# Expert weights of a mixture-of-experts block fetched by row pairs and row halves, with transposes that read every second column

## The chip, the cores and the metric

The kernel runs on one core of a Trainium2 chip. The metric is the device time of one execution in microseconds (us), taken as the median of three runs. One of the executions was also recorded by the hardware profiler; that profile and its trace are what is read here.

## What is computed

One decoder block over 512 tokens of 1024 features in float32: a norm, a pooling mixer and a gated linear recurrence side by side, an output projection, and then a mixture of experts. Each token goes to 2 of 16 experts. The last part of the reference, cut to what matters here:

```
for e in range(N_EXP):                                    # 16 experts
    he = silu(xt @ e_gate[e]) * (xt @ e_up[e])            # (512 x 1024) @ (1024 x 512), twice
    y = y + comb[:, e:e + 1] * (he @ e_down[e])           # (512 x 512) @ (512 x 1024)
x = x + y;  return rms_norm(x, norm_f_g)
```

`comb` is zero for the tokens that an expert does not get. The three matrices of an expert are 2 MB each, 96 MB for all of them.

## The kernel before

The work is done in three stages: the mixers (to about 280 us of the span), the output projection with the router (to about 370 us), and the experts (from there to the end). The change is in the experts.

**Weights.** All weights come as chunks of 1 MB, in one fixed order: gate of expert e, down of expert e-1, up of expert e. `add` (L98) describes a chunk, `load_raw` (L138) issues its load on SyncE's queue, at most 14 chunks ahead and with at most three in flight (a load waits for the landing of the third one before it). A chunk of gate or up is 512 rows of 512 columns, a chunk of down is all 512 rows of 512 of the 1024 columns; in both each partition gets four rows of 512 numbers, and each row is a run of 2 KB in memory.

**Splits.** TensorE works on float32r parts, so each half of a chunk (128 x 1024) is split in two: ScalarE casts it to the high part (`split`, L151) and VectorE subtracts that from the original, for the low part (L152). `weights` (L159) decides where in program order a split stands: three halves ahead of its use (`SPLIT_AHEAD`), and one ahead from expert 12 on (`LATE_AHEAD`).

**One expert.** The tokens of an expert sit on the 128 partitions. The loop at L791 runs, for expert e: the first half of gate e; four transposes of the hidden rows of expert e-1 (`h_parts`); the second half of gate e; `down(e - 1)`; `next_x(e + 1)`, eight transposes of the gathered rows of the next expert (`x_parts`, L713, into the tile xt); `up(e)`. Each product is three matmuls per 128 rows of weights: high by high, high by low, low by high (L726 to L728). In a matmul the tokens' tile is the stationary operand and the weights are the moving one; in a transpose the rows xg are the stationary operand and the identity is the moving one.

**Down.** `down` (L769) makes the two column halves of the result one after the other: twelve matmuls into bank py0, then ScalarE's scaled copy of py0 into y (L774), then twelve into py1 and its copy, then a scatter by GpSimd that adds y to the tokens' rows in memory. For the last expert `down` is replaced by code of its own, with the same order of halves (L890). The very last steps read the rows back, add the last expert's part, norm and store.

Each engine runs its instructions in the order in which the builder put them. Names below carry the expert (y4, py4_0) or the chunk (w60_1 is the second half of chunk 60).

Of the kernel before, what the change touches and what calls it, by code (L numbers as in the profile page):

```python
# [17 lines left out]
P = 128  # L18
S = 512
D = 1024  # L20
KD = D // P
# [8 lines left out]
DE = 512  # L30
# [6 lines left out]
def tile_hybrid_block(  # L37
# [28 lines left out]
    def bank(name):  # L66
        return psum.tile([P, 512], F32, tag="ps", name=name)
# [2 lines left out]
        return sb.tile(shape, dtype, tag=name.split("_")[0] + "_t", name=name, bufs=bufs)  # L70

    class Feat:
        """[P, KD, S] in two tiles."""

        def __init__(self, dtype, name):
            self.t = [b8([P, KD // 2, S], dtype, f"{name}{i}") for i in range(2)]
# [15 lines left out]
    tbl = tc.dram_tile([S * NE, 1], I32, name="slot_ids")  # L92
    tblw = tc.dram_tile([S * NE, 1], F32, name="slot_w")

# [1 line left out]
    chunks = []  # L96

    def add(w, r0, rows, c0, n):  # L98
        chunks.append((w[r0:r0 + rows, c0:c0 + n].rearrange("(k p) n -> p k n", p=P), rows // P, n))
        return len(chunks) - 1  # L100

    def z_chunks(base, cols):
        return [add(w_in, 0, D, base + 256 * i, 256) for i in range(cols // 256)]
# [12 lines left out]
    c_g, c_u, c_d = {}, {}, {}  # L116

    def add_exp(dst, w, e, down):
        dst[e] = [add(w[e], 0, 512, 512 * i, 512) if down else add(w[e], 512 * i, 512, 0, DE)
                  for i in range(2)]  # L120

    for e in range(NE):
        add_exp(c_g, e_gate, e, False)
# [14 lines left out]
    def load_raw(upto, after=None):  # L138
        while nxt["raw"] <= min(upto, len(chunks) - 1):
            j = nxt["raw"]  # L140
            ap, kk, n = chunks[j]
            raws[j] = b8([P, kk, n], F32, f"raw{j}")
            loads[j] = SP.dma_start(raws[j], ap).ins
            if j - IN_FLIGHT in loads:
                tc.add_manual_dep(loads[j], loads[j - IN_FLIGHT].name, SYNC, reason="loads in flight")
            if after is not None:
                tc.add_manual_dep(loads[j], after.name, SYNC, reason="loads yield to it")
            nxt["raw"] += 1
# [19 lines left out]
        load_raw((nxt["split"] - 1) // 2 + raw_ahead)  # L168
        return pairs[c]

# [1 line left out]
    x_rows = [s4([P, D], F32, f"x_rows{t}") for t in range(NT)]  # L172
    for t in range(NT):
        SP.dma_start(x_rows[t], xr[t * P:(t + 1) * P, :])
# [3 lines left out]
        SP.dma_start(raws[0][:, 4 * h:4 * h + 4], ap0[:, 4 * h:4 * h + 4])  # L178
    nxt["raw"] = 1

# [1 line left out]
    ident = const.tile([P, P], F32, name="ident")  # L182
    make_identity(nc, ident)
    mhalf = const.tile([P, 1], F32, name="mhalf")
# [21 lines left out]
    g1, lam, cb, br, bi, psc, g2f = (par[n] for n in ("g1", "lam", "cb", "br", "bi", "psc", "g2f"))  # L206
    cw = par["cw"].rearrange("p (j c) -> p j c", j=4)

# [1 line left out]
    def rstd_of(src, name):  # L210
        sq = s2([P, D], BF16, f"sq_{name}")
        ssum = tiny([P, 1], F32, f"ssum_{name}", 4)
# [37 lines left out]
            mm3(ps, w[:, 0], w[:, 1], hi[k], lo[k], k == 0, k == kk - 1)  # L250
        return ps

# [1 line left out]
    sp8 = const.tile([P, KD], F32, name="sp8")  # L254
    nsp8 = const.tile([P, KD], F32, name="nsp8")

    def softplus():
        def small(name):
            return tiny([P, KD], F32, name, 1)

        nlam, mab, ee, den, ss, s2_, acc = (small(n) for n in
                                            ("nlam", "mab", "ee", "den", "ssr", "ssq", "sacc"))
        DVE.tensor_scalar(nlam, lam, -1.0, None, op0=ALU.mult)
        DVE.tensor_tensor(mab, lam, nlam, op=ALU.min)
        ACT.activation(ee, mab, AF.Exp)
        DVE.tensor_scalar(den, ee, 2.0, None, op0=ALU.add)
        DVE.reciprocal(den, den)
        DVE.tensor_tensor(ss, ee, den, op=ALU.mult)
        DVE.tensor_tensor(s2_, ss, ss, op=ALU.mult)
        DVE.tensor_scalar(acc, s2_, 1.0 / 19.0, 1.0 / 17.0, op0=ALU.mult, op1=ALU.add)  # L270
        for k in (15, 13, 11, 9, 7, 5, 3, 1):
            DVE.tensor_tensor(acc, acc, s2_, op=ALU.mult)
            DVE.tensor_scalar(acc, acc, 1.0 / k, None, op0=ALU.add)
        DVE.tensor_tensor(acc, acc, ss, op=ALU.mult)
        DVE.tensor_scalar(nlam, nlam, 0.0, None, op0=ALU.max)
        DVE.scalar_tensor_tensor(acc, acc, 2.0, nlam, op0=ALU.mult, op1=ALU.add)
        DVE.tensor_scalar(sp8, acc, 8.0, None, op0=ALU.mult)
        DVE.tensor_scalar(nsp8, acc, -8.0, None, op0=ALU.mult)

# [1 line left out]
    ra, ix, uu = Lazy(F32, "ra"), Lazy(F32, "ix"), Lazy(F32, "uu")  # L281
    bd = []

# [45 lines left out]
            lru_gates(*pend.pop(0))  # L329
        pend.append(lru_conv(c, ps))  # L330

# [1 line left out]
    icnt = const.tile([P, PAD], F32, name="icnt")  # L333
    for j in range(PAD):
        POOL.memset(icnt[:, j:j + 1], 1.0 / (j + 1))
# [70 lines left out]
                ACT.copy(yh[cc], uu[cc])  # L406
                DVE.tensor_tensor(yl[cc], uu[cc], yh[cc].bitcast(F32), op=ALU.subtract)

# [1 line left out]
    m = Lazy(F32, "m")  # L410
    for j in range(KD):
        wp = weights(c_ga[j // 2], 4, 2)
# [13 lines left out]
        ps = feat_block(wp, (j % 2) * P, KD, xh, xl, f"zgb{j}")  # L426
        ACT.activation(sgb[j], ps, AF.Sigmoid)

# [1 line left out]
    NR = 2 * NG + NE  # L430
    rw = s2([P, KD, NG + NE], F32, "rw")
    POOL.dma_start(rw[:, :, :NG], router_group_w[0].rearrange("(k p) n -> p k n", p=P))
# [63 lines left out]
            ACT.copy(mt[i][:, 0, j, :], mj)  # L496
            DVE.tensor_tensor(mt[i][:, 1, j, :], mj, mt[i][:, 0, j, :].bitcast(F32), op=ALU.subtract)

# [1 line left out]
    x2s, h2s, xts, xpart, xg = {}, {}, {}, [], []  # L500

    def evac4(tp, hi, lo):
# [16 lines left out]
    def route(t):  # L519
# [75 lines left out]
        for e0, e1 in ((0, 2), (2, NE)) if last else ((0, 1), (1, NE)) if t == NT - 2 else ((0, NE),):  # L595
            for e in range(e0, e1):
                DVE.tensor_scalar(ohs[:, e, :], slot1, pm[:, e:e + 1], None, op0=ALU.is_equal)
                PE.matmul(spv[:, e, :3], ohs[:, e, :], idp[:, t, e, :3], start=True, stop=True)
            if last and e0 == 0:
                oh0 = s2([P, P], F32, "oh0")  # L600
                DVE.tensor_scalar(oh0, slot1, pm[:, 0:1], None, op0=ALU.is_equal)
                tps = [bank(f"xtp0_{hf}") for hf in range(2)]
                for d in range(KD):
                    PE.matmul(tps[d // 4][:, d % 4 * P:(d % 4 + 1) * P], h2s[t][:, d * P:(d + 1) * P], oh0,
                              start=True, stop=True)
            ac = slacc[:, e0:e1, :3]
            DVE.tensor_tensor(ac, ac, spv[:, e0:e1, :3], op=ALU.add)
            if t == NT - 2 and e0 == 0:
                slot_rows(rows0, e0, e1)
            if last:  # L610
                done = slot_rows(rows[:, e0:e1], e0, e1)
                if e0 == 0:
                    gather(rows[:, 1:2], xg[1])
                    with tc.issue_after(done):
                        for hf, tp in enumerate(tps):
                            hs = slice(hf * 4, hf * 4 + 4)
                            DVE.tensor_tensor(xpart[hf], tp, xpart[hf], op=ALU.add)
                            evac4(xpart[hf], xts[0][:, 0, hs, :], xts[0][:, 1, hs, :])
                    yield
# [76 lines left out]
    for hf in range(2):  # L696
        tp = bank(f"xg0t{hf}")
        for q in range(4):
            d = hf * 4 + q
            PE.transpose(tp[:, q * P:(q + 1) * P], xg[0][:, d * P:(d + 1) * P], ident)  # L700
        xpart.append(s2([P, 512], F32, f"xpart{hf}"))
        ACT.copy(xpart[hf], tp)
    xg.append(s4([P, D], F32, "xg1"))
# [9 lines left out]
    def x_parts(src, xt, nm, tp2=None):  # L713
        for hf in range(2):
            tp = bank(f"xtp{nm}_{hf}") if tp2 is None else tp2
            for q in range(4):
                d = hf * 4 + q
                PE.transpose(tp[:, q * P:(q + 1) * P], src[:, d * P:(d + 1) * P], ident)  # L718
            evac4(tp, xt[:, 0, hf * 4:hf * 4 + 4, :], xt[:, 1, hf * 4:hf * 4 + 4, :])

    def tok_mm(ps, xt, j0, wp, first, last):
        for k in range(4):
            if k % 2 == 0:
                w = wp(k // 2)
            hi, lo = xt[:, 0, j0 + k, :], xt[:, 1, j0 + k, :]
            PE.matmul(ps, hi, w[:, 0, k % 2, :], start=first and k == 0, stop=False)  # L726
            PE.matmul(ps, hi, w[:, 1, k % 2, :], start=False, stop=False)  # L727
            PE.matmul(ps, lo, w[:, 0, k % 2, :], start=False, stop=last and k == 3)  # L728

    def hidden(pg, pu, nm):  # L730
        sg = s2([P, DE], F32, f"silu{nm}")
# [36 lines left out]

    def down(e, ht):  # L769
        yt = s4([P, D], F32, f"y{e}")  # L770
        for n in range(2):
            py = bank(f"py{e}_{n}")
            tok_mm(py, ht, 0, exp_w(c_d[e], n), True, True)
            ACT.activation(yt[:, n * 512:(n + 1) * 512], py, AF.Copy, scale=wslot[:, e:e + 1])  # L774
            yield
        scatter_add(rows[:, e:e + 1], yt)

    def gate_half(e, pg, i):
        tok_mm(pg, xts[e], 4 * i, exp_w(c_g[e], i), i == 0, i == 1)

# [1 line left out]
    cn = bank("cn")  # L782
    PE.matmul(cn[:, :NE], ones, acum, start=True, stop=True)
    nmf = const.tile([P, 1], F32, name="nmf")
# [4 lines left out]
    L = NE - 1  # L789
# [26 lines left out]
    for i in range(2):  # L816
        weights(c_d[L][i], 0, 0)

# [1 line left out]
    n_max = nc.values_load(nmi[0:1, 0:1], min_val=0, max_val=S)  # L820
    with tc.If(n_max > P):
        emp = s2([P, S * NE // P], I32, "emp")
# [16 lines left out]
        with tc.For_i(0, NE, 1) as ie:  # L839
            with tc.For_i(P, S, P) as iq:  # L840
# [14 lines left out]

                def part(w, r0, c0):
                    src = w[bass.ds(ie, 1), r0:r0 + 512, c0:c0 + 512]
                    SP.dma_start(r, src.rearrange("o (k p) n -> p (o k) n", p=P))
                    for h in range(2):
                        split(r[:, 2 * h:2 * h + 2], ow[h][:, 0], ow[h][:, 1])  # L860
                    return lambda h: ow[h]
# [11 lines left out]
                    ACT.activation(og[:, n * 512:(n + 1) * 512], ps, AF.Copy, scale=wsl)  # L873
                scatter_add(sl, og)

# [1 line left out]
    xb = [b8([P, 2, D], F32, f"xb{i}") for i in range(2)]  # L877
    for t in range(NT):
        SP.dma_start(xb[t // 2][:, t % 2, :], xd[t * P:(t + 1) * P, :])  # L879
# [7 lines left out]
    xv = [[xb[t // 2][:, t % 2, n * 512:(n + 1) * 512] for n in range(2)] for t in range(NT)]  # L887
    frs = []
    py = [bank(f"py{L}_{n}") for n in range(2)]
    for n in range(2):  # L890
        tok_mm(py[n], ht, 0, exp_w(c_d[L], n), True, True)
    yp = [s4([P, 2, 512], F32R, f"yp{n}") for n in range(2)]
    for n in range(2):
        ACT.activation(yp[n][:, 0], py[n], AF.Copy, scale=wslot[:, L:L + 1])
# [56 lines left out]
```

## Time and profile before

| | |
|---|---|
| median of three runs | 697.42 us (696.87 to 699.47) |
| span of the profiled execution | 695.7 us |
| granted TensorE clock, mean | 0.977 |
| TensorE busy, share of the span | 94% |
| VectorE, ScalarE busy | 72%, 62% |
| moved by DMA | 153.23 MB |

The span goes from the first instruction to the last; the profiled execution has no other time of its own, and the span is 1.7 us under the median. Busy shares of TensorE are of limited use, because matmuls overlap each other in the record: a matmul of 512 columns is shown for 0.39 us and the next one begins 0.23 us after it. Whether it runs densely is read from the distance of the starts.

### The profile page before, as it was taken

The numbers are of one execution on the slowest core, as the hardware profiler recorded it, in microseconds if no ns is written. First come the engines' busy times: TensorE is split into PE (matmuls) and PEld (weight loads), VectorE is DVE, ScalarE is ACT, GpSimd is POOL, SyncE is SP. The second block draws the span as 40 slices with busy tenths as digits, with TensorE's granted clock in tenths as the row PEclk, the third lists the DMA queues.
The fourth block names the chain that finished last, engine by engine and source line by source line (L and its number), as shares of the span: only waits on it lengthen the run. The fifth ranks groups of instructions, "written<-read, shape, count | busy, mean of one in ns | idle before, by whom it ended". The sixth has DMA issues, their size and how long they took to land. (4 is left out here: it accounts for less than half of the span.)

```text
span 695.7 us, 8405 instructions
## 1 busy us (share of the span) xinstructions
PE 650.9 (94%) x3044; PEld 526.8 (76%) x3044; DVE 502.5 (72%) x792; ACT 431.4 (62%) x579; POOL 79.6 (11%) x101
## 2 busy tenths in 40 slices
PE   5999999999999999999959999999999999999970
PEld 4888888788888888887747787777777777777850
DVE  6886699952322227556687898898899888887946
ACT  6599957752213225141244888888888888777913
POOL 3000000000100000000131111111111111101013
PEclk9999999999999999999988999999999999999996
DMA  7920323213217113696584999999999999999134
GB/s 215 345 79 20 127 81 118 95 62 122 65 62 241 53 69 121 235 389 236 198 310 134 334 333 342 341 351 338 331 337 336 361 336 342 335 339 365 53 98 161
DMA packets 88053, 153.23 MB, mean 220 GB/s; under 512 B 7250, under 2 KB 29894, under 8 KB 88009
## 3 DMA queue, kind: packets, MB, share of 16 engines
q1 hardware_dynamic: 81736, 138.98, 57.5%
q0 software_dynamic: 5824, 12.64, 6.8%
q10 hardware_dynamic: 448, 1.05, 0.4%
q8 instruction: 24, 0.39, 0.2%
q14 instruction: 21, 0.16, 0.1%
HBM read 146.67 MB, written 14.16 MB: 231 GB/s over the span
## 5 line engine op out<-in xcount | busy, mean ns | idle before, releaser
L152 DVE TENSOR_TENSOR w<-raw,w 128x1024 fp32r<-128x1024 f32 x248 | 293.6, 1220 | 69.7 <-ACT w L151 67.6
L151 ACT CAST w<-raw 128x1024 fp32r<-128x1024 f32 x248 | 249.7, 1051 | 59.4 <-DVE w L152 14.1
L727 PE MATMUL pu<-w,xt 128*128 128x512 f32 x128 | 51.9, 406 | 2.3 <-DVE w L152 2.3
L726 PE MATMUL pu<-w,xt 128*128 128x512 f32 x128 | 52.2, 408 | 1.8 <-ACT w L151 1.8
L726 PE MATMUL pg<-w,xt 128*128 128x512 f32 x128 | 52.8, 412 | 1.1
L727 PE MATMUL py<-w,ht 128*128 128x512 f32 x128 | 51.6, 403 | 0.0
L728 PE MATMUL py<-w,ht 128*128 128x512 f32 x128 | 50.7, 396 | 0.6 <-DVE ht L505 0.6
L728 PE MATMUL pg<-w,xt 128*128 128x512 f32 x128 | 50.4, 394 | 0.5 <-DVE xt L505 0.5
L728 PE MATMUL pu<-w,xt 128*128 128x512 f32 x128 | 50.7, 396 | 0.0
L727 PE MATMUL pg<-w,xt 128*128 128x512 f32 x128 | 50.3, 393 | 0.3 <-DVE w L152 0.3
L508 POOL DMA_INDIRECT xg<-h_rows,rows x16 | 26.9, 1679 | 197.6 <-PE xtp L718 177.8
L726 PE MATMUL py<-w,ht 128*128 128x512 f32 x128 | 48.8, 395 | 0.8 <-ACT ht L504 0.8
L743 POOL DMA_INDIRECT x_acc<-y,rows x15 | 24.6, 1639 | 62.9 <-ACT y L774 36.4
L727 PEld LDWEIGHTS pu<-w,xt 128*128 128x128 f32 x128 | 24.5, 191 | 8.8 <-DVE w L152 3.2
L726 PEld LDWEIGHTS pg<-w,xt 128*128 128x128 f32 x128 | 24.1, 188 | 9.4 <-ACT w L151 5.3
L726 PEld LDWEIGHTS pu<-w,xt 128*128 128x128 f32 x128 | 24.3, 190 | 7.7 <-ACT w L151 3.1
L726 PEld LDWEIGHTS py<-w,ht 128*128 128x128 f32 x128 | 24.5, 191 | 6.1 <-ACT ht L504 1.0
L505 DVE TENSOR_TENSOR xt<-xtp,xt 128x512 fp32r<-128x512 f32 x30 | 19.4, 686 | 13.4 <-ACT xt L504 13.4
L727 PEld LDWEIGHTS pg<-w,xt 128*128 128x128 f32 x128 | 24.1, 188 | 6.2 <-DVE w L152 0.7
L728 PEld LDWEIGHTS py<-w,ht 128*128 128x128 f32 x128 | 24.4, 191 | 5.7 <-DVE ht L505 1.0
L728 PEld LDWEIGHTS pg<-w,xt 128*128 128x128 f32 x128 | 24.0, 188 | 5.8 <-DVE xt L505 1.1
L728 PEld LDWEIGHTS pu<-w,xt 128*128 128x128 f32 x128 | 24.5, 191 | 4.8
(292 smaller groups left out, 1414.6 us busy)
## 6 DMA issues: line engine op xcount, KB each, us to landing
raw<-in_exp_w_gate_dram SPq DMA_DIRECT2D x32, 1024.0 KB, 8.0
raw<-in_exp_w_up_dram SPq DMA_DIRECT2D x32, 1024.0 KB, 7.9
raw<-in_exp_w_down_dram SPq DMA_DIRECT2D x32, 1024.0 KB, 10.7
raw<-in_w_in_dram SPq DMA_DIRECT2D x17, 1024.0 KB, 7.7
raw<-in_proj_b_dram SPq DMA_DIRECT2D x4, 1024.0 KB, 9.3
raw<-in_w_out_dram SPq DMA_DIRECT2D x4, 1024.0 KB
x_rows<-in_x_dram SPq DMA_DIRECT2D x4, 512.0 KB
xrow<-in_x_dram SPq DMA_DIRECT2D x4, 512.0 KB
```

What stands on the lines that cost most here:

```text
L151: ACT.copy(hi, r)
L152: DVE.tensor_tensor(lo, r, hi.bitcast(F32), op=ALU.subtract)
L505: DVE.tensor_tensor(lo, tv, hi.bitcast(F32), op=ALU.subtract)
L508: return POOL.indirect_dma_start(out=dst, out_offset=None, in_=h2d[:n, :], in_offset=bass.IndirectOffsetOnAxis(ap=idx, axis=0), bounds_che ...
L726: PE.matmul(ps, hi, w[:, 0, k % 2, :], start=first and k == 0, stop=False)
L727: PE.matmul(ps, hi, w[:, 1, k % 2, :], start=False, stop=False)
L728: PE.matmul(ps, lo, w[:, 0, k % 2, :], start=False, stop=last and k == 3)
L743: POOL.indirect_dma_start(out=xd, out_offset=bass.IndirectOffsetOnAxis(ap=idx, axis=0), in_=src, in_offset=None, bounds_check=S - 1, oob_i ...
```

## The change

Four things change, in the experts alone. A chunk of gate or up is read so that a partition takes two neighbouring rows at a time, 4 KB in one run (`pairs_of`), twice per chunk. So the rows of weights that meet in one matmul are now every second one of a block of 256, and the tokens' features have to be in the same order: `x_cols` reads every second column of xg in each transpose, and of the router's h2 in one matmul per block. A chunk of down is now 256 rows of all 1024 columns, again 4 KB runs. And since a chunk of down then holds half of the rows for both halves of the result, `down` fills py0 and py1 together, chunk by chunk (`down_mm`), and ScalarE's two copies come after all of it.

```
+    def pairs_of(w):
+        return w.rearrange("(j p t) n -> p j (t n)", p=P, t=2)
+    def x_cols(src, d):
+        return src[:, d // 2 * 2 * P + d % 2:d // 2 * 2 * P + 2 * P:2]
...
-        dst[e] = [add(w[e], 0, 512, 512 * i, 512) if down else add(w[e], 512 * i, 512, 0, DE)
-                  for i in range(2)]
+        dst[e] = []
+        for i in range(2):
+            if down:
+                dst[e].append(add(w[e], 256 * i, 256, 0, D))
+            else:
+                chunks.append((pairs_of(w[e][512 * i:512 * i + 512]), 4, DE))
+                dst[e].append(len(chunks) - 1)
...
-                PE.transpose(tp[:, q * P:(q + 1) * P], src[:, d * P:(d + 1) * P], ident)
+                PE.transpose(tp[:, q * P:(q + 1) * P], x_cols(src, d), ident)
...
+    def down_mm(pys, ht, i, wp):
+        for q in range(2):
+            w = wp(q)
+            k = 2 * i + q
+            for n, ps in enumerate(pys):
+                hi, lo = ht[:, 0, k, :], ht[:, 1, k, :]
+                w_h, w_l = (w[:, j, 0, n * 512:(n + 1) * 512] for j in range(2))
+                PE.matmul(ps, hi, w_h, start=k == 0, stop=False)
+                PE.matmul(ps, hi, w_l, start=False, stop=False)
+                PE.matmul(ps, lo, w_h, start=False, stop=k == 3)
...
     def down(e, ht):
         yt = s4([P, D], F32, f"y{e}")
-        for n in range(2):
-            py = bank(f"py{e}_{n}")
-            tok_mm(py, ht, 0, exp_w(c_d[e], n), True, True)
+        pys = [bank(f"py{e}_{n}") for n in range(2)]
+        for i in range(2):
+            down_mm(pys, ht, i, exp_w(c_d[e], i))
+            if i == 0:
+                yield
+        for n, py in enumerate(pys):
             ACT.activation(yt[:, n * 512:(n + 1) * 512], py, AF.Copy, scale=wslot[:, e:e + 1])
-            yield
         scatter_add(rows[:, e:e + 1], yt)
...
-    for n in range(2):
-        tok_mm(py[n], ht, 0, exp_w(c_d[L], n), True, True)
+    for i in range(2):
+        down_mm(py, ht, i, exp_w(c_d[L], i))
```

On TensorE, in loop 5 of the experts, these rows of the kernel before are the middle of `down(4)` (w58 and w59 are the two chunks of its weights):

```order
L726 MATMUL py4_0_3932<-w58_1_3911,ht4_3903 128x512
L726 MATMUL py4_1_3954<-w59_0_3920,ht4_3903 128x512
L727 MATMUL py4_0_3932<-w58_1_3911,ht4_3903 128x512
L728 MATMUL py4_0_3932<-w58_1_3911,ht4_3903 128x512
L726 MATMUL py4_0_3932<-w58_1_3911,ht4_3903 128x512
L727 MATMUL py4_0_3932<-w58_1_3911,ht4_3903 128x512
L728 MATMUL py4_0_3932<-w58_1_3911,ht4_3903 128x512
L727 MATMUL py4_1_3954<-w59_0_3920,ht4_3903 128x512
L728 MATMUL py4_1_3954<-w59_0_3920,ht4_3903 128x512
L726 MATMUL py4_1_3954<-w59_0_3920,ht4_3903 128x512
```

py4_0 is complete after 13 of the 24 matmuls of down. In the changed kernel the end of `down(4)` on TensorE reads like this, up to the first matmul of up (pu5):

```order
L753 MATMUL py4_0_3932<-w59_1_3934,ht4_3903 128x512
L753 MATMUL py4_1_3933<-w59_1_3934,ht4_3903 128x512
L734 MATMUL xtp6_0_3980<-ident_81,xg0_2905 128x128 x4
L754 MATMUL py4_0_3932<-w59_1_3934,ht4_3903 128x512
L755 MATMUL py4_0_3932<-w59_1_3934,ht4_3903 128x512
L754 MATMUL py4_1_3933<-w59_1_3934,ht4_3903 128x512
L755 MATMUL py4_1_3933<-w59_1_3934,ht4_3903 128x512
L734 MATMUL xtp6_1_3987<-ident_81,xg0_2905 128x128 x4
L742 MATMUL pu5_3997<-w60_0_3943,xt_5_3820 128x512
```

py4_0 is now complete only after 22 of the 24, with two matmuls and four transposes between its end and the first matmul of up.

On ScalarE, in the same loop, the changed kernel has the same instructions in the same places as the kernel before; these are the rows of the changed one (L167 is the cast that was L151, L804 the copy into y that was L774, L520 the copy into xt that was L504; w60 and w61 are the chunks of up 5, w62 the first chunk of gate 6):

```order
L759 ACTIVATE silu5_4038<-pg5_3882 128x512
L167 CAST w59_1_3934<-raw59_3553 128x1024
L167 CAST w60_0_3943<-raw60_3577 128x1024
L804 ACTIVATE y4_3931<-py4_0_3932,wslot_1896 128x512
L167 CAST w60_1_3954<-raw60_3577 128x1024
L167 CAST w61_0_3963<-raw61_3605 128x1024
L804 ACTIVATE y4_3931<-py4_1_3933,wslot_1896 128x512
L520 CAST xt_6_3979<-xtp6_0_3980 128x512
L520 CAST xt_6_3979<-xtp6_1_3987 128x512
L167 CAST w61_1_3998<-raw61_3605 128x1024
L167 CAST w62_0_4007<-raw62_3628 128x1024
```

Nothing moved here: the copy of py4_0 still stands ahead of the casts w60_1 and w61_0. In loop 12, where splits are taken one half ahead, the rows did move. Before:

```order
L151 CAST w101_1_5060<-raw101_4666 128x1024
L774 ACTIVATE y11_5036<-py11_0_5037,wslot_1896 128x512
L151 CAST w102_0_5069<-raw102_4690 128x1024
L504 CAST xt_13_5084<-xtp13_0_5085 128x512
L774 ACTIVATE y11_5036<-py11_1_5059,wslot_1896 128x512
L504 CAST xt_13_5084<-xtp13_1_5092 128x512
L151 CAST w102_1_5103<-raw102_4690 128x1024
```

and in the changed kernel:

```order
L167 CAST w101_1_5059<-raw101_4666 128x1024
L167 CAST w102_0_5068<-raw102_4690 128x1024
L804 ACTIVATE y11_5036<-py11_0_5037,wslot_1896 128x512
L804 ACTIVATE y11_5036<-py11_1_5038,wslot_1896 128x512
L520 CAST xt_13_5084<-xtp13_0_5085 128x512
L520 CAST xt_13_5084<-xtp13_1_5092 128x512
L167 CAST w102_1_5103<-raw102_4690 128x1024
```

Both copies into y now stand one behind the other, right ahead of the copies into xt and of the cast w102_1.

## Rows read from the trace of the kernel before

**Rows 1.** Stretch 450 to 500 us: each engine's busy time (instructions), clock, DMA share, GB/s.

```profile
450.00:500.00 50.00, 49.66 (x233) 39.79 (x232) 45.10 (x45) 42.32 (x50) 10.34 (x6) 1.00 0.99 339
```

**Rows 2.** TensorE in loops 4 and 5: start, us shown, line, names, count.

```profile
452.58 0.48 PE L726 MATMUL pu<-w,xt 128*128 128x512 f32 x1
...
464.57 0.39 PE L726 MATMUL py<-w,ht 128*128 128x512 f32 x1
...
468.88 0.81 PE L718 MATMUL xtp<-ident,xg 128*128 128x128 f32 x6
...
470.46 0.39 PE L728 MATMUL py<-w,ht 128*128 128x512 f32 x1
...
470.82 0.48 PE L726 MATMUL pu<-w,xt 128*128 128x512 f32 x1
...
475.51 0.50 PE L726 MATMUL pg<-w,xt 128*128 128x512 f32 x1
```

**Rows 3.** Waits from 403 to 585 us: total us, times, longest.

```profile
ACT xt L504 <- PE pu L728: 9.2, 10, 0.9
...
PEld pg L726 <- ACT w L151: 5.3, 10, 0.5
```

**Rows 4.** Waits of SyncE's queue from 403 to 585 us.

```profile
SPq L143 <- DMA raw<-in_exp_w_gate_dram: 48.3, 18, 5.7
```

**Rows 5.** SyncE's issues: a pair in loop 4, the last three weight loads, what waits for them.

```profile
448.38 3.04 SPq L143 DMA_DIRECT2D raw<-in_exp_w_up_dram  x2
...
632.32 5.71 SPq L143 DMA_DIRECT2D raw<-in_exp_w_down_dram  x3
646.36 0.35 SPq L881 DMA_DIRECT2D gfb<-in_norm_f_g_dram  x1
```

**Rows 6.** ScalarE: the last four casts of weights.

```profile
656.52 3.89 ACT L151 CAST w<-raw 128x1024 fp32r<-128x1024 f32 x4
```

**Rows 7.** ScalarE in loop 5; in brackets the idle time before, and what ended it.

```profile
468.03 0.69 ACT L774 ACTIVATE y<-py,wslot 128x512 f32<-128x512 f32 x1
468.85 2.01 ACT L151 CAST w<-raw 128x1024 fp32r<-128x1024 f32 x2
470.89 0.69 ACT L774 ACTIVATE y<-py,wslot 128x512 f32<-128x512 f32 x1
472.50 1.08 ACT L504 CAST xt<-xtp 128x512 fp32r<-128x512 f32 x2 [0.92 <-PE pu L728]
473.46 2.00 ACT L151 CAST w<-raw 128x1024 fp32r<-128x1024 f32 x2
```

**Rows 8.** VectorE in loop 5.

```profile
469.94 2.36 DVE L152 TENSOR_TENSOR w<-raw,w 128x1024 fp32r<-128x1024 f32 x2 [0.36 <-ACT w L151]
```

**Rows 9.** Loop 13: ScalarE's copy of py1, and TensorE around it.

```profile
617.85 0.69 ACT L774 ACTIVATE y<-py,wslot 128x512 f32<-128x512 f32 x1 [1.45 <-PE py L728]
...
620.50 0.49 PE L726 MATMUL pu<-w,xt 128*128 128x512 f32 x1 [0.75 <-ACT w L151]
...
621.76 0.50 PE L727 MATMUL pu<-w,xt 128*128 128x512 f32 x1 [0.77 <-DVE w L152]
```

**Rows 10.** After the last `down`: ScalarE's copy into y, GpSimd's last scatter, SyncE's read of the rows.

```profile
663.88 0.69 ACT L774 ACTIVATE y<-py,wslot 128x512 f32<-128x512 f32 x1 [3.47 <-PE py L728]
...
664.85 2.35 POOL L743 DMA_INDIRECT x_acc<-y,rows  x1 [22.80 <-DVE w L152]
...
673.24 1.78 SPq L879 DMA_DIRECT2D xb<-x_acc  x4
```

**Rows 11.** One line's instructions: ns min/median/max, first and last start, form.

```profile
L718 PEld LDWEIGHTS xtp<-ident,xg x120: 137/139/143, 379.9 to 639.4; 128*128 128x128 f32 x120
```

**Rows 12.** Stretches as in Rows 1: loads of 4 KB runs, of 2 KB runs, TensorE in loop 13.

```profile
4.00:6.00 2.00, 0.00 (x0) 0.00 (x0) 0.96 (x6) 1.71 (x3) 0.94 (x5) 1.00 1.04 391
283.00:290.00 7.00, 7.00 (x33) 5.79 (x32) 3.21 (x8) 0.90 (x4) 0.00 (x0) 1.00 1.00 380
622.90:626.40 3.50, 3.50 (x10) 2.73 (x9) 3.17 (x3) 2.54 (x3) 0.00 (x0) 0.51 1.04 339
```

More of the change, by code (lines that the diff above doesn't have):

```diff
@@ L142, in load_raw @@
             raws[j] = b8([P, kk, n], F32, f"raw{j}")
-            loads[j] = SP.dma_start(raws[j], ap).ins
+            dst = raws[j]
+            if ap.shape[1] != kk:
+                dst = dst.rearrange("p (j t) n -> p j (t n)", t=kk // ap.shape[1])
+            loads[j] = SP.dma_start(dst, ap).ins
             if j - IN_FLIGHT in loads:
@@ L603, in route @@
                 for d in range(KD):
-                    PE.matmul(tps[d // 4][:, d % 4 * P:(d % 4 + 1) * P], h2s[t][:, d * P:(d + 1) * P], oh0,
+                    PE.matmul(tps[d // 4][:, d % 4 * P:(d % 4 + 1) * P], x_cols(h2s[t], d), oh0,
                               start=True, stop=True)
@@ L699, in tile_hybrid_block @@
             d = hf * 4 + q
-            PE.transpose(tp[:, q * P:(q + 1) * P], xg[0][:, d * P:(d + 1) * P], ident)
+            PE.transpose(tp[:, q * P:(q + 1) * P], x_cols(xg[0], d), ident)
         xpart.append(s2([P, 512], F32, f"xpart{hf}"))
@@ L857, in part @@
                     src = w[bass.ds(ie, 1), r0:r0 + 512, c0:c0 + 512]
-                    SP.dma_start(r, src.rearrange("o (k p) n -> p (o k) n", p=P))
+                    if w is e_down:
+                        SP.dma_start(r, src.rearrange("o (k p) n -> p (o k) n", p=P))
+                    else:
+                        SP.dma_start(r.rearrange("p (j t) n -> p j (t n)", t=2),
+                                     src.rearrange("o (j p t) n -> p (o j) (t n)", p=P, t=2))
                     for h in range(2):
```

## The prediction

> **What bounds the kernel now.** I read the busy shares by stretch first. In the steady part of the expert stage TensorE is shown busy for 49.66 of 50 us and the DMA engines for 0.99 of the time [rows 1]. Both look like the bound, and only one can be, so I read next how densely the matmuls start. From the first matmul of down to the first of up, 24 matmuls and 8 transposes take 470.82 - 464.57 = 6.25 us [rows 2]. A transpose takes (0.81 - 0.27) / 5 = 0.108 us: six are shown as 0.81 us, the last of them for about 0.27 us. That leaves (6.25 - 0.87) / 24 = 0.224 us for a matmul, and there is no room between them. One loop takes 470.82 - 452.58 = 18.24 us from up to up [rows 2].
>
> Then the waits of this part. No engine waits for a load of weights; the only TensorE wait is 0.5 us per loop for a cast of ScalarE, ten times [rows 3]. The loads wait for each other, three in flight [rows 4], a pair being issued within 3.04 us, so about 2.67 us apart (0.37 us of it is the second issue) [rows 5]. Does their pace reach the compute? The last three are issued from 632.32 on, and what waits for the last of them goes at 646.36 [rows 5]; ScalarE's last four casts begin at 656.52, those of the last chunk half way through, at about 658.4 [rows 6]. The loads are 12 us early at their latest point. So the DMA engines are nearly always busy and yet bound nothing. The bound is TensorE's row of matmuls, with ScalarE's and VectorE's splits close behind it: both are in order, and busy for 42.32 and 45.10 of 50 us [rows 1].
>
> **The loads.** 4 KB runs halve the number of packets. Where x is loaded in 4 KB runs at the start, the engines move 391 GB/s at a share of 1.04, so 376 per full share; with 2 KB runs they move 380 at 1.00 [rows 12]. By these rows a load gets neither faster nor slower by more than a few per cent. I take zero effect, because nothing waits for a load. A slowdown would have to use up the 12 us first: 5% on the 240 us of loading since 400 us. For the other sign I keep a rival.
>
> [...]
>
> **The strided transposes.** In a transpose the tile xg is the stationary operand, so the step of two falls on the weight load, shown for 139 ns at a distance of 108 ns, 120 times [rows 11]; 8 transposes of the first rows and 16 matmul rows of the router are read in the same way. No row of this trace has a TensorE operand with a step, so the cost is open: below, nothing, since the same number of elements is read and no fewer can be; above, twice the 108 ns, when each pair of neighbours costs as much as two. That is 0.108 x 144 = 15.5 us at most, less where it falls into a wait. I take zero, since only half of the columns is skipped, and keep the upper end as a rival.
>
> [...]
>
> **Down by row halves.** The matmuls are as many as before, and so are casts, copies and scatters. What moves is when py0 is complete. Before, that is after 13 of down's 24 matmuls: 464.57 + 13 x 0.227 = 467.5 us, and ScalarE's copy of it at 468.03 comes without a wait [rows 7]. Now two matmuls and four transposes stand between the end of py0 and the first of up, at 470.82. So its last matmul starts at 470.82 - 0.43 - 3 x 0.227 = 469.71. A copy follows the start of its last matmul by 470.89 - 470.46 = 0.43 us, as py1's shows [rows 2, 7]: 470.14 us, 2.11 us later than 468.03. ScalarE is in order and its order has not changed here, so it sits before this copy, with two casts for up behind it.
>
> From there ScalarE's chain runs without a gap, by the rows of the same loop [rows 7]: copy of py0 0.69 (to 470.83), two casts 2.01 (472.84), copy of py1 0.69 (473.53), both copies into xt 472.50 to 473.46, so 0.96 (474.49), then two casts 2.00, to 476.49. The last of these is the first cast of the next gate. Before, it was done at 475.46, and TensorE's matmul that needs it (pg, which the builder has put ahead of up's last five) went at 475.51 [rows 2, 7]. Now it goes at 476.54, **1.03 us later**. The 0.92 us that the copy into xt waited for a buffer before is eaten up in this.
>
> On the way a first wait appears: the first cast behind py0's copy is done at 471.88, VectorE's part takes 2.36 / 2 = 1.18 us [rows 8], to 473.06, and up's eighth matmul wanted it at 470.82 + 0.09 + 7 x 0.227 = 472.5. TensorE stands there for some 0.55 us, and in front of pg for 0.75 instead of 0.3. From pg to the next down nothing is late, as before. So the loop becomes 18.24 + 1.03 = 19.3 us.
>
> Counted up: loops 2 to 11 (the ten of [rows 3]) 10.3 us; loop 1, whose splits start with more in hand, between 0 and 1, I take 0.5. In loops 12 to 14 the copies into y stand behind each other. In loop 13 py1's copy waited until 617.85 [rows 9]; py0 is now complete 0.45 us before py1, so its copy runs from 617.40, py1's ends at 617.40 + 2 x 0.69 = 618.78 instead of 618.54, and the two waits of TensorE behind it (before 620.50 and before 621.76, shown as 0.75 and 0.77 of idle time; from start to start the second is 1.26 - 0.23 = 1.03) grow by 0.24. The same for loop 14. In loop 12 the first copy into xt also falls behind them, another 0.48: 0.7. Together 1.2 us. After the last down the scatter goes once both copies are done [rows 10], by the same step 0.24 us later; the read of the rows and the end follow it. The last expert's own down is hidden: the rows are read from 673.24 on, and it has about 7 us until they are there.
>
> Sum: 10.3 + 0.5 + 1.2 + 0.2 = **12.2 us**. Against the profiled execution that is 695.7 + 12.2 = 707.9; the median of the runs is 1.7 above that span, so 697.4 + 12.2 = **709.6 us**, 1.7% slower.
>
> **Rivals.**
> *ScalarE has slack enough.* If py0's late copy only moves its idle time, the time is 697.4 us. For it: 7.7 of 50 us idle. Against it: 18.24 x 42.32 / 50 = 15.4 us of work per loop, and the chain above uses the idle time and still ends 1.03 us late.
> *The loads do set the end, and get faster.* The long waits of loops 12 to 14, about 2 us each by those of loop 13 [rows 9], and the stretch at half the clock behind them (3.5 us at a granted 0.51 cost 3.5 x 0.49 = 1.7 us [rows 12]) vanish if they are due to late loads: 697.4 - 3 x 2 - 1.7 = 690 us. It decides once a cast is held by a landing. Against it: those waits name casts, not loads, and the landing leads by 12 us [rows 5, 6, 9].
> *The step of two is paid.* Doubled weight loads of the transposes add up to 15.5 us, part of it in waits that are there anyway: 718 to 725 us.
> [...]
>
> **How the numbers follow.** Forecast 0.70 (its own range 705 to 715: 9 to 15 us, by 0.3 us per loop either way, and the clock once or twice more); no change 0.10; loads 0.04; step of two 0.12; clock 0.04. Faster by over 0.5% (3.5 us; about what a measurement of this kernel can tell from no change): 0.04; within: 0.11, with the forecast at its weakest; slower: 0.85. The range 703 to 722 leaves out most of the no-change case, the loads and the clock.
>
> **What would show it.** Right: loops of about 19.3 us; some eleven waits of about 2 us of ScalarE's copy into y for py; TensorE waiting in each loop for a low part in up and for a cast at pg; loads still not waited for. The weight loads of the strided transposes stay at 139 ns; at 200 and more the third rival is true. Wrong: loops of 18.2 us, or a cast that waits for a landing.

## The result, and the profile after

The changed kernel takes 706.09 us (median of four runs, 704.01 to 706.75) against 697.90 for the kernel before: a ratio of 1.0121, 95% interval 1.0100 to 1.0142. It is 1.2% slower, by 8.2 us; forecast were 709.6 us. The span of the profiled execution is 704.8 us, 9.1 more than before.

TensorE in loops 4 and 5 of the changed kernel, the counterpart of [rows 2] (start, us shown, line, names, count; in brackets the idle time before, and what ended it):

```profile
457.01 0.47 PE L742 MATMUL pu<-w,xt 128*128 128x512 f32 x1
...
474.25 0.63 PE L734 MATMUL xtp<-ident,xg 128*128 128x128 f32 x4
...
474.95 0.39 PE L755 MATMUL py<-w,ht 128*128 128x512 f32 x1
...
476.03 0.47 PE L742 MATMUL pu<-w,xt 128*128 128x512 f32 x1
476.35 0.39 PE L743 MATMUL pu<-w,xt 128*128 128x512 f32 x1
...
477.50 0.40 PE L742 MATMUL pu<-w,xt 128*128 128x512 f32 x1
478.31 0.50 PE L743 MATMUL pu<-w,xt 128*128 128x512 f32 x1 [0.41 <-DVE w L168]
478.64 0.39 PE L744 MATMUL pu<-w,xt 128*128 128x512 f32 x1
...
480.94 0.39 PE L742 MATMUL pu<-w,xt 128*128 128x512 f32 x1
481.45 0.50 PE L742 MATMUL pg<-w,xt 128*128 128x512 f32 x1
481.79 0.49 PE L743 MATMUL pu<-w,xt 128*128 128x512 f32 x1
482.12 0.39 PE L744 MATMUL pu<-w,xt 128*128 128x512 f32 x1
```

A loop now takes 476.03 - 457.01 = 19.02 us instead of 18.24. A wait in up is where it was forecast: up's eighth matmul (478.31) starts 0.81 us after the seventh, 0.58 more than the usual 0.227. It costs a little more than that, because the next one follows 0.33 us later and not 0.227. Before pg (481.45) the row waits 0.51 - 0.227 = 0.28 us, about as in the kernel before, where pg starts 475.51 - 475.02 = 0.49 us after the matmul ahead of it.

Waits of the changed kernel from 403 to 595 us, which hold ten such loops (total us, times, longest); they answer to [rows 3]:

```profile
DVE w L168 <- ACT w L167: 27.7, 20, 2.3
ACT y L804 <- PE py L755: 21.1, 10, 2.1
...
PEld pu L743 <- DVE w L168: 8.5, 10, 0.8
...
PEld pg L742 <- ACT w L167: 5.4, 10, 0.6
```

ScalarE stands 2.1 us for py0 in each loop, a wait that the kernel before did not have; VectorE stands behind ScalarE's cast, and TensorE behind VectorE. What ScalarE does then, in loop 5 (answers to [rows 7]):

```profile
475.37 0.69 ACT L804 ACTIVATE y<-py,wslot 128x512 f32<-128x512 f32 x1 [2.11 <-PE py L755]
475.96 1.99 ACT L167 CAST w<-raw 128x1024 fp32r<-128x1024 f32 x2
477.85 0.68 ACT L804 ACTIVATE y<-py,wslot 128x512 f32<-128x512 f32 x1
478.43 1.07 ACT L520 CAST xt<-xtp 128x512 fp32r<-128x512 f32 x2
479.37 2.03 ACT L167 CAST w<-raw 128x1024 fp32r<-128x1024 f32 x2
```

From the copy of py0 to the end of the cast that pg needs (the second of the last row) there is no gap. Each of these instructions starts before the one ahead is shown to end: the copy is shown for 0.69 us, and the next cast begins 0.59 us after it.

The loads: SyncE's waits from 403 to 585 us (answers to [rows 4]), and a stretch of the steady part (answers to [rows 1], columns as there):

```profile
SPq L159 <- DMA raw<-in_exp_w_down_dram: 42.9, 17, 3.3
SPq L159 <- DVE w L168: 39.9, 27, 3.2
SPq L159 <- PE pu L744: 31.5, 20, 1.7
...
SPq L159 <- DMA raw<-in_exp_w_gate_dram: 2.7, 5, 0.6
```

```profile
450.00:500.00 50.00, 48.52 (x223) 38.66 (x221) 41.69 (x43) 39.43 (x48) 9.23 (x6) 1.00 0.98 363
```

The loads move 363 GB/s in this stretch instead of 339, and wait more for buffers (DVE, PE) and less for landings. Still nothing waits for a load of weights. The transposes' weight loads are dearer (ns min/median/max; [rows 11] had 139):

```profile
L734 PEld LDWEIGHTS xtp<-ident,xg x120: 195/202/214, 381.9 to 649.1; 128*128 128x128 f32 x120
```

### The profile page after: what moved, and what is told of

Same layout as the page of the kernel before. It is cut to its first block, busy times and chain, and to the rows that moved or that the text cites. A ratio compares the mean times of both kernels' runs of the same rounds, so it can differ in the third digit from the quotient of the medians.

```text
span 704.8 us, 8407 instructions
## 1 busy us (share of the span) xinstructions
PE 653.3 (93%) x3044; PEld 526.5 (75%) x3044; DVE 500.2 (71%) x792; ACT 428.7 (61%) x579; POOL 75.9 (11%) x101
## 3 DMA queue, kind: packets, MB, share of 16 engines
q1 hardware_dynamic: 57160, 138.98, 54.8%
## 5 line engine op out<-in xcount | busy, mean ns | idle before, releaser
L167 ACT CAST w<-raw 128x1024 fp32r<-128x1024 f32 x248 | 249.2, 1052 | 56.7 <-DVE w L168 14.6
L754 PE MATMUL py<-w,ht 128*128 128x512 f32 x128 | 50.9, 398 | 0.0
L755 PE MATMUL py<-w,ht 128*128 128x512 f32 x128 | 50.0, 391 | 0.6 <-DVE ht L521 0.6
L753 PE MATMUL py<-w,ht 128*128 128x512 f32 x128 | 46.3, 391 | 0.8 <-ACT ht L520 0.8
L804 ACT ACTIVATE y<-py,wslot 128x512 f32<-128x512 f32 x30 | 20.4, 686 | 34.1 <-PE py L755 34.1
L524 POOL DMA_INDIRECT xg<-h_rows,rows x16 | 18.6, 1161 | 201.1 <-PE xtp L734 181.2
L743 PEld LDWEIGHTS pu<-w,xt 128*128 128x128 f32 x128 | 24.1, 188 | 17.1 <-DVE w L168 11.7
L770 POOL DMA_INDIRECT x_acc<-y,rows x15 | 29.2, 1944 | 70.9 <-ACT y L804 47.5
L742 PEld LDWEIGHTS pu<-w,xt 128*128 128x128 f32 x128 | 24.3, 190 | 7.9 <-ACT w L167 3.3
L753 PEld LDWEIGHTS py<-w,ht 128*128 128x128 f32 x128 | 24.0, 188 | 5.9 <-ACT ht L520 1.0
L755 PEld LDWEIGHTS py<-w,ht 128*128 128x128 f32 x128 | 24.1, 188 | 5.6 <-DVE ht L521 1.1
L754 PEld LDWEIGHTS py<-w,ht 128*128 128x128 f32 x128 | 24.2, 189 | 4.5
```

The source lines that it names most:

```text
L167: ACT.copy(hi, r)
L524: return POOL.indirect_dma_start(out=dst, out_offset=None, in_=h2d[:n, :], in_offset=bass.IndirectOffsetOnAxis(ap=idx, axis=0), bounds_che ...
L753: PE.matmul(ps, hi, w_h, start=k == 0, stop=False)
L754: PE.matmul(ps, hi, w_l, start=False, stop=False)
L755: PE.matmul(ps, lo, w_h, start=False, stop=k == 3)
L770: POOL.indirect_dma_start(out=xd, out_offset=bass.IndirectOffsetOnAxis(ap=idx, axis=0), in_=src, in_offset=None, bounds_check=S - 1, oob_i ...
```

## The experiments

The theory after the result: the copy of py0, which stands ahead of two casts in ScalarE's order, comes late since py0 is complete late; that is nearly all of the loss. The rivals: the strided transposes carry it (their weight load did rise), the new loads do, or the new order of matmuls does by itself. Loops below are means over the ten from the first matmul of up 2 to that of up 12. In the kernel before these are

```profile
416.14 0.48 PE L726 MATMUL pu<-w,xt 128*128 128x512 f32 x1
...
598.50 0.48 PE L726 MATMUL pu<-w,xt 128*128 128x512 f32 x1
```

and in the changed kernel, with up 13 as a third row,

```profile
418.95 0.47 PE L742 MATMUL pu<-w,xt 128*128 128x512 f32 x1
...
609.32 0.47 PE L742 MATMUL pu<-w,xt 128*128 128x512 f32 x1
...
629.37 0.47 PE L742 MATMUL pu<-w,xt 128*128 128x512 f32 x1
```

so 18.24 and 19.04 us.

### Down by column halves again (e1)

```
-                dst[e].append(add(w[e], 256 * i, 256, 0, D))
+                dst[e].append(add(w[e], 0, 512, 512 * i, 512))
...
         yt = s4([P, D], F32, f"y{e}")
-        pys = [bank(f"py{e}_{n}") for n in range(2)]
-        for i in range(2):
-            down_mm(pys, ht, i, exp_w(c_d[e], i))
...
+        for n in range(2):
+            py = bank(f"py{e}_{n}")
+            tok_mm(py, ht, 0, exp_w(c_d[e], n), True, True)
+            ACT.activation(yt[:, n * 512:(n + 1) * 512], py, AF.Copy, scale=wslot[:, e:e + 1])
+            yield
```

> The changed kernel with down as before: chunks of 512 columns, py0 made first. Row pairs of gate and up (4 KB) and the transposes that read every second column stay. If the late copy of py0 is what costs (my theory): ScalarE's copy into y waits no longer, the wait of up for a low part goes, loops of 18.3 us, 697 to 700 us in all, of which the strided transposes are about 1 us (14 loops x two groups of four, each 0.035 us longer than before by the starts in the changed kernel). If the strided transposes or the 4 KB loads carry the loss (rivals): loops stay near 19.0 us, 704 to 707 us.

Measured: 697.87 us, ratio to before 1.0004 (0.9981 to 1.0027). First matmuls of up 2 and up 12:

```profile
417.50 0.48 PE L742 MATMUL pu<-w,xt 128*128 128x512 f32 x1
...
600.64 0.48 PE L742 MATMUL pu<-w,xt 128*128 128x512 f32 x1
```

That is 18.31 us per loop, as expected, and no wait of a copy into y for py. So the loss comes with down by row halves. Pairs of rows and strided transposes together cost 0.07 us per loop and give nothing.

### Down by row halves alone (e2)

The kernel before, with the new chunks of down, `down_mm`, and the copies at its end; gate, up and the transposes stay.

```
-        dst[e] = [add(w[e], 0, 512, 512 * i, 512) if down else add(w[e], 512 * i, 512, 0, DE)
+        dst[e] = [add(w[e], 256 * i, 256, 0, D) if down else add(w[e], 512 * i, 512, 0, DE)
```

> The kernel before with one part of the change alone: down by row halves, py0 and py1 filled together. Gate and up in 2 KB runs, transposes of whole blocks. My theory: ScalarE's copy into y waits some 2 us for py0 in each loop, up waits about 0.6 us for a low part, loops of 18.9 to 19.0 us, 704 to 706 us. Rivals (strided transposes, or 4 KB runs of gate and up, carry the loss): loops of 18.2 to 18.3 us, 697 to 699 us.

Measured: 706.10 us, ratio 1.0106 (1.0071 to 1.0140). ScalarE and TensorE in it:

```profile
474.54 0.69 ACT L788 ACTIVATE y<-py,wslot 128x512 f32<-128x512 f32 x1 [2.07 <-PE py L739]
```

```profile
475.16 0.47 PE L726 MATMUL pu<-w,xt 128*128 128x512 f32 x1
...
477.48 0.51 PE L727 MATMUL pu<-w,xt 128*128 128x512 f32 x1 [0.46 <-DVE w L152]
...
494.16 0.47 PE L726 MATMUL pu<-w,xt 128*128 128x512 f32 x1
```

The whole loss is there with this part alone: both waits, and loops of 19.01 us.

### py0 earlier: second chunk of down to py0 first (e4)

All matmuls of py0 in the second chunk stand ahead of py1's, and the transposes of x and up behind all of down.

```
-        for q in range(2):
...
+        for q, n in (((0, 0), (0, 1), (1, 0), (1, 1)), ((0, 0), (1, 0), (0, 1), (1, 1)))[i]:
...
+            with tc.issue_after(last) if i and n else nullcontext():
                 PE.matmul(ps, hi, w_h, start=k == 0, stop=False)
...
-            next_x(e + 1)
-        hh = hidden(pg, up(e), f"{e}")
+        with tc.issue_after(nxt["py0"]) if 0 < e < L else nullcontext():
+            if 0 < e < L:
+                next_x(e + 1)
+            pu = up(e)
+        hh = hidden(pg, pu, f"{e}")
```

> The changed kernel, with the second chunk of down used up for py0 before py1, and the transposes of x after all of it: py0 is complete after 18 of 24 matmuls instead of 22, so its copy comes about 1.4 us earlier against the first matmul of up (six matmuls and eight transposes stand between, 2.5 us, instead of two and four). My theory: the copy's wait falls from 2.1 to about 0.7 us, the wait in up (0.58 us) is gone since it is smaller than 1.4 us, the wait before pg stays about 0.3: loops of 18.3 us, 697 to 700 us. If the loss came from the strides or the loads: loops of 19.0 us, 704 to 707 us.

Measured: 696.67 us, ratio 0.9987 (0.9966 to 1.0008). From its waits, 403 to 595 us:

```profile
ACT y L808 <- PE py L757: 11.3, 10, 1.1
...
PEld py L756 <- DVE w L168: 5.6, 10, 0.6
```

The copy's wait is halved to 1.1 us (0.7 expected), and the wait in up is gone: up 2 and up 12 start at 416.84 and 599.34 us, loops of 18.25 us. One thing was not expected: the last quarter of down's weights is now wanted three matmuls earlier and isn't split by then, so TensorE waits for it (the second row); the wait before pg has vanished in return.

### The copies behind the casts (e5)

TensorE's order is that of the changed kernel; only ScalarE's two copies into y move.

```
-        ACT.copy(hi, r)
+        nxt["cast"] = ACT.copy(hi, r).ins
...
-        for n, py in enumerate(pys):
-            ACT.activation(yt[:, n * 512:(n + 1) * 512], py, AF.Copy, scale=wslot[:, e:e + 1])
+        with tc.issue_after(nxt["cast"]):
+            for n, py in enumerate(pys):
+                ACT.activation(yt[:, n * 512:(n + 1) * 512], py, AF.Copy, scale=wslot[:, e:e + 1])
```

> The changed kernel, with ScalarE's two copies into y placed behind the two casts for up that they stood in front of; TensorE's order is not touched, py0 is as late as in the changed kernel. My theory: the two casts no longer queue behind a copy that waits, so the wait in up for a low part goes, though a copy still waits for py0: loops of 18.3 us (18.24 and 0.07 for the strides), 697 to 700 us. A wait before pg of 0.3 to 0.5 us stays, since both copies now stand ahead of the copies into xt. If it is not the queue on ScalarE but TensorE's own new order, the strides or the loads: loops of 19.0 us, 704 to 707 us.

Measured: 698.87 us, ratio 1.0009 (0.9989 to 1.0030). ScalarE in loop 5:

```profile
469.14 2.00 ACT L167 CAST w<-raw 128x1024 fp32r<-128x1024 f32 x2 [0.71 <-PE py L755]
471.04 1.26 ACT L805 ACTIVATE y<-py,wslot 128x512 f32<-128x512 f32 x2
472.86 1.07 ACT L520 CAST xt<-xtp 128x512 fp32r<-128x512 f32 x2 [0.56 <-PE pu L744]
```

Up 2 and up 12 start at 416.32 and 599.21 us: loops of 18.29 us. The casts run while py0 is still being made, and the copies come without any wait, better than expected. This settles it: py0's last matmul starts 1.08 us before the first of up in both (470.11 and 471.19 us here, 474.95 and 476.03 in the changed kernel), and TensorE does the same work in the same order; the loss came from what stood behind the copy on ScalarE.

### 4 KB runs without the step (e6), and a step of four (e7)

Two variants of the first experiment. In one, `x_cols` gives whole blocks again, while the weights stay in pairs of rows; it does the same work, but features meet other rows of weights, so what it computes is not the block. In the other, four rows go to a partition.

```
-        return src[:, d // 2 * 2 * P + d % 2:d // 2 * 2 * P + 2 * P:2]
+        return src[:, d * P:(d + 1) * P]
```

> The run with down by column halves once more (e1), with transposes that read whole blocks of 128 columns; so the features of a token meet other rows of gate and up than they should, and all work is as before. What is left of the change is the 4 KB runs of gate and up. My theory: loops of 18.24 us as in the kernel before, the weight loads of the transposes back at 139 ns, 1 us less than e1 by the 0.07 us per loop, and no more; that is under what the medians can tell (696 to 698 us), so the loops are read from the trace. If the step of two costs nothing, loops stay at 18.31 us; if the 4 KB loads help by themselves, loops are below 18.24 us.

```
-        return w.rearrange("(j p t) n -> p j (t n)", p=P, t=2)
+        return w.rearrange("(j p t) n -> p j (t n)", p=P, t=4)
...
-        return src[:, d // 2 * 2 * P + d % 2:d // 2 * 2 * P + 2 * P:2]
+        return src[:, d // 4 * 4 * P + d % 4:d // 4 * 4 * P + 4 * P:4]
...
```

> e1 with the dose doubled: four neighbouring rows of gate and up per partition (8 KB runs), and transposes that read every fourth column; down by column halves. If the price of the step grows with the memory that is passed over (0.035 us per group of four transposes at a step of two): 0.07 to 0.2 us more per loop, loops of 18.4 to 18.5 us, weight loads shown for well over 202 ns, 699 to 701 us. If any step costs the same: 18.31 us and 202 ns again, 698 us. If longer runs help the loads and the loads matter, it is faster than e1; my theory says that they don't, at whatever length.

Measured: 696.55 us, ratio 1.0001 (0.9986 to 1.0017), without the step; 699.42 us, 1.0028 (1.0009 to 1.0048), with a step of four. Weight loads of the transposes without the step:

```profile
L734 PEld LDWEIGHTS xtp<-ident,xg x120: 137/139/143, 380.7 to 638.7; 128*128 128x128 f32 x120
```

and with a step of four:

```profile
L734 PEld LDWEIGHTS xtp<-ident,xg x120: 197/208/212, 382.8 to 642.2; 128*128 128x128 f32 x120
```

Up 2 and up 12 start at 416.97 and 599.34 us without the step, at 419.35 and 602.79 us with a step of four: loops of 18.24 and 18.34 us, against 18.31 with a step of two. So a step costs 0.07 us per loop, and double the step adds 0.03: the expectation that the price grows with the step (18.4 and more) fell. The time with a step of four, 699.42 us, does lie in the range of that expectation (699 to 701), but not because of the loops: of the 2.5 us by which its profile is longer than that of the first experiment, 1.9 lie ahead of the first matmul of up 0 (381.43 against 379.56 us), and whether the step has a part in those is not shown. Runs of 4 KB (two thirds of the chunks) leave the loop where it was. From 403 to 585 us the loads move 341 GB/s in the kernel before, 346 with 4 KB runs for down alone (e2), 347 and 348 with 4 KB runs for gate and up (e1 and the run without the step), 354 with both (the changed kernel), and 352 with 8 KB runs for gate and up; it is not needed.

### The late loops (e8, e9)

In loops 12 to 14 up waits for a cast and a low part in every version so far. These two kernels let the splits of the last experts stand three halves ahead, one on top of "py0 earlier", one on the kernel before.

```
-    SPLIT_AHEAD, LATE_AHEAD, RAW_AHEAD = 3, 1, 14
+    SPLIT_AHEAD, LATE_AHEAD, RAW_AHEAD = 3, 3, 14
```

> e4 (py0 first in the second chunk) with the splits of the last four experts three halves ahead instead of one. In e4, loops 12 to 14 take 19.5 us instead of 18.25, with waits of up of 0.5 and 1.03 us for a cast and a low part. If these come from splits that stand too late in the order: they vanish, 3 x 1.25 = 3.7 us less than e4, 693 us. Rival: with three ahead the casts wait for buffers or for the last loads instead, and the time stays at 697 us or rises.

> The kernel before with that same edit alone (three halves ahead to the end), so that what e8 gains can be put down to the change or not. If the waits of loops 12 to 14 come from the order of the splits: loops of 18.24 us there instead of 19.6 and 21.4, 1.4 + 1.4 + 1.4 us less, some 693 us, and the same gain as e8 against e4. If the 4 KB runs are needed for it (loads too late at 2 KB): the casts wait for landings here, and not in e8; 697 us.

Measured: 691.75 us, ratio 0.9920 (0.9902 to 0.9938), and 692.58 us, 0.9928 (0.9913 to 0.9943). First matmuls of up 12 to 15 in the first:

```profile
601.93 0.48 PE L742 MATMUL pu<-w,xt 128*128 128x512 f32 x1
...
620.14 0.47 PE L742 MATMUL pu<-w,xt 128*128 128x512 f32 x1
...
637.96 0.47 PE L742 MATMUL pu<-w,xt 128*128 128x512 f32 x1
...
652.18 0.39 PE L742 MATMUL pu<-w,xt 128*128 128x512 f32 x1
```

and in the kernel before with the edit:

```profile
600.09 0.48 PE L726 MATMUL pu<-w,xt 128*128 128x512 f32 x1
...
618.34 0.48 PE L726 MATMUL pu<-w,xt 128*128 128x512 f32 x1
```

Both beat both kernels of this study. The gain has nothing to do with the change: it comes with 2 KB runs as well, so the waits of these loops were a matter of where the splits stood, not of late loads.

### The smallest repair (e10)

Against the kernel with py0 first and the splits ahead (e8), down's matmuls go back to the order of the changed kernel; py0's last three still stand ahead of py1's, and the transposes behind all of down.

```
-        for q, n in (((0, 0), (0, 1), (1, 0), (1, 1)), ((0, 0), (1, 0), (0, 1), (1, 1)))[i]:
+        for q, n in ((0, 0), (0, 1), (1, 0), (1, 1)):
...
-            with tc.issue_after(last) if i and n else nullcontext():
+            with tc.issue_after(last) if i and q + n else nullcontext():
```

> e8 with the order of matmuls in down as in the changed kernel, and only the transposes of x moved: all eight behind down, and py0's last three matmuls ahead of py1's. py0 is now complete after 21 of 24 matmuls, with three matmuls and eight transposes up to the first of up: its last matmul starts 4 x 0.227 + 8 x 0.115 = 1.83 us before that instead of 1.08, so the copy comes 0.75 us earlier than in the changed kernel. That is just more than the 0.58 us for which up stood. If the time at which the copy runs is all that counts: the wait in up is gone, the copy still waits about 1.3 us, no new wait in down (its weights are used in the old order), the wait before pg is 0.25 to 0.3 us again: loops of 18.3 us, 691 to 693 us. If the order of matmuls by row halves costs by itself: a wait in up or loops of 18.6 us and more, 695 us and more.

Measured: 694.49 us, ratio 0.9973 (0.9954 to 0.9992); the profiled execution has a span of 691.3 us. From its waits, 403 to 595 us:

```profile
ACT y L808 <- PE py L757: 14.0, 10, 1.4
...
PEld pg L742 <- ACT w L167: 5.6, 11, 0.7
```

and the copy of py0 in loop 5, where up starts at 472.03 us:

```profile
470.67 0.69 ACT L808 ACTIVATE y<-py,wslot 128x512 f32<-128x512 f32 x1 [1.39 <-PE py L757]
```

No wait is left in up or in down, the wait before pg is back, and up 2 and up 12 start at 416.94 and 600.77 us: loops of 18.38 us. The copy runs 472.03 - 470.67 = 1.36 us before up instead of 0.66: 0.70 us earlier was enough to remove a wait of 0.58, though it still waits 1.4 us itself. By the mark set before the run (18.6 us and more) the order by row halves costs nothing of its own. But the loops are 0.07 us longer than in the first experiment, and where these come from is not shown. The median is 1.5 to 3.5 us above the expected 691 to 693, and 2.7 above that of e8. The loops explain most of this: from the first matmul of up 0 to that of up 14 this kernel takes 637.50 - 378.47 = 259.0 us, e8 637.96 - 380.95 = 257.0.

## Why the prediction was right, and where it was off

**The mechanism** held up to the wait in up: py0's copy at 0.66 us before the first matmul of up (forecast 470.82 - 470.14 = 0.68), waits of 2.1 us in ten loops, and a wait in up of 0.58 (0.55). The longer wait before pg did not come. Undoing that part removes the loss; that part alone brings it; taking the casts out from behind the copy removes it with TensorE's order kept.

**The term that was too large** is ScalarE's chain from py0's copy to pg: 1.03 us per loop. I summed shown durations, 470.14 to 476.54 = 6.40 us. In the trace of after it takes 481.45 - 475.37 = 6.08, since ScalarE's instructions overlap by about 0.1 us each. That is 0.32 less, so the wait before pg stayed at 0.28 instead of growing to 0.75. With 0.07 for the transposes and some hundredths because the copy starts 0.66 us before up and not 0.68, 1.03 becomes the measured 0.80 (from 18.24 to 19.04, mean of loops 2 to 11). Over ten loops that is 8.0 us instead of 10.3, the larger part of the error.

**The transposes.** I took zero, with 0.108 us each as upper bound. The weight load did go to 202 ns, for which I had said that the third rival would be true at 200 and more. That reading was wrong: the shown time rose by 63 ns, while the loop rose by 0.07 us for eight of them, 0.009 each, about 1 us in all by the first experiment and the one without the step. With down by row halves most of even that falls into the wait (19.01 us per loop without the step in e2, where the copy starts 475.16 - 474.54 = 0.62 us before up, and 19.04 with it, where it starts 0.66 before). The zero was my own estimate, shown by no row of the kernel before. The trace shows 202 ns for a step of two against 139 without one, and 208 for a step of four (e7); a step of two shows 209 in e8, where all eight transposes stand in a row. The price is small either way, 0.07 and 0.10 us per loop.

**The loads** were hidden, as assumed. The profile counts 57160 packets on their queue instead of 81736. From 403 to 585 us they moved 4% more (354 GB/s instead of 341), and nothing came of it.

**The ends.** Loop 1 grew from 17.70 to 18.39 us, 0.69 (0.5 taken). The late loops: 0.44, -1.55 and -0.09, where I had 1.2 in all. The -1.55 is the stretch at a granted clock of 0.51 [rows 12], which the profile of before has in loop 13 and that of after has not; the run with the copies behind the casts has one at 0.55 in loop 12:

```profile
603.50:607.30 3.80, 3.80 (x12) 2.96 (x11) 3.05 (x3) 1.61 (x2) 0.00 (x0) 0.55 0.99 361
```

So it came after these waits in some executions and not in others: in loop 13 of the changed kernel, with waits of 0.69 and 0.76 us, the granted clock was 1.00 (629.37 to 649.24 us). The first experiment, whose loop 13 is as long, is the better measure: its loops 12 to 14 take 19.74, 19.87 and 15.88 us, those of the changed kernel 20.05, 19.87 and 15.91. Loop 12 lost 0.31 us (0.7 forecast), and the 0.24 forecast for each of loops 13 and 14 did not come. In loop 13 of the changed kernel, with up at 629.37:

```profile
628.47 1.27 ACT L804 ACTIVATE y<-py,wslot 128x512 f32<-128x512 f32 x2 [1.87 <-PE py L755]
629.62 1.07 ACT L520 CAST xt<-xtp 128x512 fp32r<-128x512 f32 x2
```

The first copy starts 0.90 us before up, where I had 618.11 - 617.40 = 0.71, and the two take 1.15 us from start to start, not 2 x 0.69; so the copies into xt start 0.25 us after up, no later than in the kernel before (618.43 - 618.11 = 0.32). In part it is the same fault as in the chain above.

The tail is 0.5 us shorter, where a loss of 0.2 was forecast; from the first matmul of up 15 to the end the kernels profiled here take 39.0 to 41.8 us, so neither can be read from it. Against these gains the first matmul of up 0 comes 1.96 us later in the profile of after. That is spread: four kernels that do the same as the changed one up to there (e4, e5, e8, e10) have it at 378.38 to 380.95 us. Sum of the profiles: 1.96 + 0.16 (loop 0) + 0.69 + 8.0 + 0.44 - 1.55 - 0.09 - 0.52 = 9.1 us. Neither the 1.96 nor the -1.55 is shown to come from the change, and it is luck that they nearly cancel.

**The rivals** that ended elsewhere: slack on ScalarE was not enough; the waits of the late loops did vanish, but by placing splits earlier and not by faster loads. A clock that falls more often has 0.04 in the forecast and "once or twice more" in its range; no run shows this in the loops with the new wait: from 403 to 585 us the granted clock was 1.00, in the changed kernel and in e2.

## What to carry to other kernels

When a result is spread over two accumulators that finish together, look at who reads them and what stands behind those readers in the order of their engine: here a copy that nobody was in a hurry for waited 2.1 us and held up two casts that TensorE needed. Place such a copy behind the urgent work, or let the accumulator finish a few matmuls sooner; either gave the 1.2% back, within what the runs can tell (ratios to before of 1.0009 and 0.9987). And take chains on one engine from the distance of starts in the trace, not from shown durations (6.08 us against 6.40 here).

## What the runs showed of the hardware

- The weight load of a stationary operand in float32 that is read with a step of two is shown for 202 ns (the changed kernel), 205 (e1) and 209 (e8) instead of 139, with a step of four for 208 (e7); the loop of eight such transposes grows by only 0.07 and 0.10 us (18.31 in e1 and 18.34 in e7, against 18.24 in e6).
- In loop 5 of the changed kernel, after a wait of TensorE for its weights, the first matmul is followed by the next at 0.33 us instead of 0.227 (478.31 to 478.64), and before pg the one behind it as well (481.45, 481.79, 482.12). So in these rows a wait costs 0.1 to 0.2 us more than its length. The first matmul after the transposes shows 0.32 too (476.03 to 476.35), though no wait is shown there.
- On ScalarE, in loop 5 of the changed kernel, an instruction starts about 0.1 us before the one ahead is shown to end: a copy shown for 0.69 us takes 0.59 from start to start (475.37 to 475.96).
- From 403 to 585 us the loads moved 341 GB/s at a DMA share of 0.99 with 2 KB runs (the kernel before), and 354 at 0.98 with 4 KB runs (the changed kernel).
